# A two-layer attention block: the first layer's opening rebuilt on 128-column tiles, and a modulation chunk moved behind the queries

## The chip, the cores and the metric

The kernel runs on one core of one Trainium2 chip. The number that counts is the device time of one execution in microseconds (us); three runs of the kernel before gave 1213.51, 1214.17 and 1214.43 us, and their median is the time that is compared.

## What is computed

The input is one sequence of 1024 tokens by 1024 channels and two layers. Each layer normalises the tokens, scales and shifts them with a modulation that comes from a second input `c`, projects them to 2736 columns, runs three mixers on these (a retention, a latent attention with rotary positions, a gated linear attention), and adds the gated result. All arithmetic is float32.

```python
c_act = silu(c)
for l in range(2):
    shift, scale, gate = split(c_act @ ada_w[l] + ada_b[l], 3)     # 1024 columns each
    h = rms_norm(x, norm_w[l]) * (1 + scale) + shift
    proj = h @ w_in[l]                  # 1024 x 2736
    r_o = retention(rope(rq), rope(rk), rv)
    m_o = mla(mq, mkv, mkr, ...)        # latent attention
    g_o = gla(gq, gk, gv, gg)           # gated linear attention
    mixed = concat(rms_norm(r_o) * silu(rz), m_o * silu(mz), rms_norm(g_o) * silu(gz))
    x = x + gate * (mixed @ w_out[l])
return rms_norm(x, final_norm)
```

## The kernel before

The activations are kept transposed: `x[k]` is a tile of 128 channels by 1024 tokens, k from 0 to 7, and work goes in two token halves of 512 (`hf`). A float32 product is made of three faster ones (`mm3`, L535 to L537): both operands are split into a rounded part and a remainder (`split`, L435 on ScalarE and L436 on GpSimd or VectorE), and TensorE adds high by high, high by low and low by high. So each projection of 128 output columns is 2 halves x 8 k x 3 matmuls of 512 columns.

`start()` is the opening of the first layer. It is written in a manual schedule: each engine runs its instructions in the order in which the code states them, and waits in that order. It loads x, the tables of positions, the weights of three projections (`rq1`, `rq2`, `rk1`) and 16 tiles of the modulation matrix `ada_w`, all from SyncE's queue, each load 512 KB. Sums of squares over channels go to TensorE as a matmul with ones (`ssq`, L274), and the inverse root is a guess by ScalarE's logarithm and exponential (L424, L425) with one Newton step of three VectorE instructions (L429 to L431). The modulation is made in chunks of 512 columns: chunks 0 and 1 are the shift, 2 and 3 the scale. Chunk 0 is a row on TensorE (`ada_row`, L619, L625). Chunks 1 and 2 are sums over eight row blocks, each multiplied by a column of silu(c) (`ada_steps`: ScalarE L588 and GpSimd L590 for some blocks, VectorE L592 for others), turned into columns by TensorE (L580). Chunk 3 is a product of each column with silu(c) laid along the row (`silrow`), summed by VectorE as it goes (`ada`, L560). GpSimd multiplies x by the inverse root for k 0 to 3 (L320). `h_first` (L798 to L800) then makes h for k 0 to 3 and `make_h` (L666, L672, L679) for k 4 to 7, and the three projections run k 0 to 3 first, then k 4 to 7, half by half. The angles of the rotary tables are made on VectorE at the very start (`trig_angles`), ScalarE takes their sines (`trig`, with two loads of its function table), and SyncE writes the tables to memory (L331).

After the opening only TensorE's order is manual; the other engines' orders come from a planner that places instructions by estimated times. The first layer goes on with `ret_prep` (rotary step on rq and rk, projection `rk2`), `mkv`, `mq0`, `mq1` with their norms (`lat_norm`), `rv`, the keys (`mla_keys`), the retention core, the queries (`mla_queries`, in two parts around `rz0`), `rz1`, then the search for row maxima (`mla_max`), which opens with loads on SyncE's queue (L1251 to L1252, L1198 to L1202). The remaining modulation chunks (gates of both layers, shift and scale of the second) are made one at a time by `ada` at places named by letters: `next_chunk("a")` to `next_chunk("q")` does a chunk if its letter is in `CHUNKS`. A chunk is eight tiles of 256 KB through three buffers, each a load on SyncE's queue (L557) and a product on VectorE (L560), and these products keep their order among themselves.

## Time and profile before

| | |
|---|---|
| time, median of three runs | 1214.17 us |
| the profiled execution's own time | 1211.83 us |
| its span, first to last instruction | 1210.0 us |
| TensorE busy | 1127.9 us, 93% of the span |
| VectorE busy | 853.9 us, 71% |
| ScalarE busy | 564.7 us, 47% |
| GpSimd busy | 559.1 us, 46% |
| mean granted TensorE clock | 0.978 |

The profiled execution is 2.34 us faster than the median of the runs, and 1.83 us of its time lie outside the span. Busy times are sums over the whole span; the opening takes the first 90 us of it and looks different from the rest.

### The profile page before, as it was taken

The numbers are of one execution on the slowest core, as the hardware profiler recorded it, in microseconds if no ns is written. First come the engines' busy times: TensorE is split into PE (matmuls) and PEld (weight loads), VectorE is DVE, ScalarE is ACT, GpSimd is POOL, SyncE is SP. The second block draws the span as 40 slices with busy tenths as digits, with TensorE's granted clock in tenths as the row PEclk, the third lists the DMA queues.
The fourth block names the chain that finished last, engine by engine and source line by source line (L and its number), as shares of the span: only waits on it lengthen the run. The fifth ranks groups of instructions, "written<-read, shape, count | busy, mean of one in ns | idle before, by whom it ended". The sixth has DMA issues, their size and how long they took to land.

```text
span 1210.0 us, 16960 instructions
## 1 busy us (share of the span) xinstructions
PE 1127.9 (93%) x5928; PEld 932.3 (77%) x5928; DVE 853.9 (71%) x1449; ACT 564.7 (47%) x1096; POOL 559.1 (46%) x483
## 2 busy tenths in 40 slices
PE   6599999999999999998998989989999999999996
PEld 1378787778887788886777879777888778888896
DVE  7977779647778666778866565964777766685764
ACT  5432442343453477873444234233345447886421
POOL 3824324443443355683554431544344334568630
PEclk9789999899999999999999999999999999999999
DMA  9806565272117744229451452627212563423722
GB/s 362 283 20 181 172 200 174 88 228 66 41 53 196 177 110 101 68 105 323 146 191 70 121 176 98 221 89 233 61 41 57 162 157 92 105 62 124 276 88 70
DMA packets 65585, 169.01 MB, mean 140 GB/s; under 512 B 10262, under 2 KB 13334, under 8 KB 65500
## 3 DMA queue, kind: packets, MB, share of 16 engines
q1 hardware_dynamic: 65500, 167.93, 45.2%
q8 instruction: 47, 0.77, 0.3%
q14 instruction: 38, 0.31, 0.1%
HBM read 125.36 MB, written 38.41 MB: 135 GB/s over the span
## 4 chain that ended last, share of the span: by engine, by line
PE 59%; DVE 21%; DMA 7%; issue 5%; ACT 4%; POOL 3%; SPq 1%; DVEq 0%; POOLq 0%; ACTq 0%
DMA ada_aw<-awc 3%; PE wo_pspj L535 3%; PE wo_pspj L537 3%; PE wo_pspj L536 3%; PE mhead_psacc L1346 3%; PE mhead_psacc L1344 3%; PE mhead_psacc L1345 3%; DVE ada_aw L560 3%; PE pmz_pspj L535 2%; PE pmz_pspj L536 2%; PE pmz_pspj L537 2%; DVE mmax_mx L1296 2%; PE mhead_pss L1312 2%; PE mhead_pss L1313 2%; DMA aw<-awk 2%
## 5 line engine op out<-in xcount | busy, mean ns | idle before, releaser
L535 PE MATMUL wo_pspj<-gran_mx,wwo_wh 128*128 128x512 f32 (+1 forms) x240 | 89.6, 373 | 6.7 <-DVE ssq_x L1423 3.8
L537 PE MATMUL wo_pspj<-gran_mx,wwo_wl 128*128 128x512 f32 (+1 forms) x240 | 88.4, 368 | 0.0
L536 PE MATMUL wo_pspj<-gran_mx,wwo_wh 128*128 128x512 f32 (+1 forms) x240 | 88.3, 368 | 0.0
L436 POOL TENSOR_TENSOR wwo_wl<-wwo_wst,wwo_wh 128x1024 fp32r<-128x1024 f32 x27 | 69.3, 2569 | 40.1 <-ACT wwo_wh L435 40.0
L1296 DVE TENSOR_REDUCE mmax_mx<-mmax_psmm 128x1 f32<-128x512 f32 (+1 forms) x96 | 57.4, 598 | 31.5 <-PE mmax_psmm L1294 30.4
L1321 POOL TENSOR_TENSOR mhead_wh<-mhead_p,mhead_wh 128x384 fp32r<-128x384 f32 (+1 forms) x48 | 57.9, 1207 | 38.9 <-DVE mhead_wh L1320 38.9
L560 DVE SCALAR_TENSOR_TENSOR ada_aw<-ada_aw,silrow 128x512 f32<-128x512 f32 x64 | 57.2, 919 | 24.6 <-DMA ada_aw<-awc 24.3
L1296 DVE TENSOR_REDUCE mmax_mx<-mmax_psacc 128x1 f32<-128x256 f32 (+2 forms) x96 | 48.9, 509 | 20.8 <-PE mmax_psacc L1294 19.5
L1326 DVE TENSOR_TENSOR mhead_ph<-mhead_pss,mhead_ph 128x512 fp32r<-128x512 f32 x48 | 33.1, 689 | 37.4 <-ACT mhead_pss L1325 36.8
L535 PEld LDWEIGHTS wo_pspj<-gran_mx,wwo_wh 128*128 128x128 f32 x240 | 45.2, 188 | 16.7 <-issue 6.0
L535 PE MATMUL pmz_pspj<-mkh_h,wmz_wh 128*128 128x512 f32 x128 | 52.7, 412 | 0.0
L1321 POOL TENSOR_TENSOR mhead_wl<-mhead_p,mhead_wl 128x128 fp32r<-128x128 f32 (+1 forms) x48 | 35.8, 746 | 34.0 <-DVE mhead_wl L1320 34.0
L537 PEld LDWEIGHTS wo_pspj<-gran_mx,wwo_wl 128*128 128x128 f32 x240 | 45.2, 188 | 7.5
L536 PEld LDWEIGHTS wo_pspj<-gran_mx,wwo_wh 128*128 128x128 f32 x240 | 45.3, 189 | 7.5 <-issue 0.2
L536 PE MATMUL pmz_pspj<-mkh_h,wmz_wh 128*128 128x512 f32 x128 | 50.4, 394 | 0.0
L537 PE MATMUL pmz_pspj<-mkh_h,wmz_wl 128*128 128x512 f32 x128 | 50.1, 392 | 0.0
L639 ACT ACTIVATE ssq_sq<-ssq_x 128x512 f32<-128x512 f32 (+1 forms) x31 | 16.6, 534 | 51.6 <-DVE ssq_x L1423 51.5
L535 PE MATMUL pv_pspj<-wrv_wh,mkh_h 128*128 128x304 f32 x128 | 40.4, 316 | 0.0
L644 DVE TENSOR_TENSOR ssq_sq<-ssq_sq,ssq_sq 128x512 f32<-128x512 f32 (+1 forms) x30 | 30.0, 1000 | 14.4 <-ACT ssq_sq L639 14.4
L1294 PE MATMUL mmax_psmm<-mmax_mxk,mmax_mxq 104*128 104x512 f32 (+1 forms) x96 | 34.8, 362 | 5.6 <-DVE mmax_mx L1296 2.7
L536 PE MATMUL pv_pspj<-wrv_wl,mkh_h 128*128 128x304 f32 x128 | 38.7, 302 | 0.0
L537 PE MATMUL pv_pspj<-wrv_wh,mkh_h 128*128 128x304 f32 x128 | 38.4, 300 | 0.0
(522 smaller groups left out, 4001.1 us busy)
## 6 DMA issues: line engine op xcount, KB each, us to landing
ada_aw<-awc SPq DMA_DIRECT2D x64, 256.0 KB
wwo_wst<-wo SPq DMA_DIRECT2D x32, 512.0 KB
aw<-awk SPq DMA_DIRECT2D x12, 512.0 KB
x<-xT SPq DMA_DIRECT2D x8, 512.0 KB
kn<-mk_ph SPq DMA_DIRECT2D x16, 256.0 KB
kn<-mk_pl SPq DMA_DIRECT2D x16, 256.0 KB
qn<-mq_ph SPq DMA_DIRECT2D x16, 256.0 KB
qn<-mq_pl SPq DMA_DIRECT2D x16, 256.0 KB
```

The lines of the kernel that those rows point to most:

```text
L436: (eng or nc.gpsimd).tensor_tensor(lo, src, hi.bitcast(F32), ALU.subtract)
L535: mm(ps, lh, rh, start=start, stop=False)
L536: mm(ps, lh, rl, start=False, stop=False)
L537: self.last = mm(ps, ll, rh, start=False, stop=stop)
L560: step = nc.vector.scalar_tensor_tensor(v, v, 1.0, self.silrow[:, cs], ALU.mult, ALU.mult, accum_out=t[:, n * j + i:n * j + i + 1])
L1294: nc.tensor.matmul(ps[:, :w], st["q"][0:104, 128 * i:128 * i + 128], st["k"][0:104, 512 * j:512 * j + w], start=True, stop=True)
L1296: nc.vector.tensor_reduce(mx[:, i, j:j + 1], ps[:, :w], AX.X, ALU.max)
L1321: nc.gpsimd.tensor_tensor(pl, p, ph.bitcast(F32), ALU.subtract)
L1326: nc.vector.tensor_tensor(pl, s, ph.bitcast(F32), ALU.subtract)
L1344: mm(acc[:, o], vh, ph, start=(j == 0), stop=False, skip_group_check=True)
L1345: mm(acc[0:64, o], vl, ph, start=False, stop=False, skip_group_check=True)
L1346: mm(acc[:, o], vh, pl, start=False, stop=last, skip_group_check=True)
```

## The change

`start()` is rewritten. The modulation tiles now hold 128 output columns each with all 1024 rows: tile k gives shift and scale of channels 128k to 128k+127, just what `x[k]` needs. The loads come in the order x, then for each k the weights of a projection (k below 3), the scale tile and the shift tile. ScalarE squares all of x, tile by tile; VectorE adds the squares in pairs. The sine work moves from the start to a place behind k = 2, and its last two steps from GpSimd to ScalarE. The root is ScalarE's guess and its square with two VectorE instructions for each half. `column(k)` makes scale (VectorE, a product with `silrow`) and shift (for k below 5 eight one-column matmuls on TensorE, for the others a second VectorE product); `make(k)` makes h for both halves, with `column(k + 1)` between its two parts. Each k's matmuls follow it at once, for those projections whose weights are there (`behind`). GpSimd has no work in the opening. The four old helpers (`ada_steps`, `ada_load`, `ada_row`, `h_first`) go away. `CHUNKS` changes from "acdkno" to "cfgkno": in the first layer the chunks at a (behind `ret_prep`) and d (behind the norm of the latents) go, and there are chunks at f (between the two parts of the queries) and g (behind `rz1`, ahead of `mla_max`); in the second layer, which has two chunks left, they move from a and c to c and f.

```diff
@@ constants @@
-CHUNKS = "acdkno"
+CHUNKS = "cfgkno"
+SHIFT_PE = 5
@@ host_layout @@
-    A["awk"] = ada_w[0].reshape(4, 2, 128, 6, 512)[:, :, :, :3].transpose(3, 0, 2, 1, 4).reshape(3, 4, 128, 1024)
-    A["awc"] = ada_w.transpose(0, 2, 1).reshape(L * 6, 4, 128, D)[3:]
+    A["aws"] = ada_w[0][:, :128 * SHIFT_PE].reshape(KT, 128, SHIFT_PE, 128).transpose(2, 1, 0, 3).reshape(SHIFT_PE, 128, D)
+    A["awc"] = ada_w.transpose(0, 2, 1).reshape(L * 6, 4, 128, D)
@@ start @@
-        dma(pos, A["pos"])
         dma(self.vec, A["vec"])
+        dma(self.cst("ident"), A["cst"][:, 0:128])
         for k in range(KT):
             dma(self.x[k], A["xT"][k])
...
+            if k == 1:
+                dma(pos, A["pos"])
         names = ("rq1", "rq2", "rk1")
-        wst = {}
...
-        aw = self.ada_load((0, 2))
-        for n in names:
-            w_load(n)
-        aw.update(self.ada_load((1, 3)))
+        wst, aw = {}, {}
+        for k in range(KT):
+            if k < len(names):
+                wst[names[k]] = self.sl(name="wst")
+                dma(wst[names[k]], A["wi"][0, MIDX[names[k]]])
+            aw[k] = [self.sl(name="aw") for _ in range(2)]
+            dma(aw[k][1], A["awc"][2 + k // 4, k % 4])
+            dma(aw[k][0], A["aws"][k] if k < SHIFT_PE else A["awc"][k // 4, k % 4])
         self.ahead()
...
+        nc.scalar.preload_act_table_set(TABLES)
...
-        ang, kk, s = self.trig_angles(pos)
-        self.lab = "ssq_"
-        total(square(0), first=True)
-        q1 = square(1, P)
-        q2 = square(2, V)
-        self.trig(ang, kk, s)
-        add(q1, q2)
         o = VO["c"]
         self.silu(self.silc, self.vec[:, o:o + KT], self.sm([128, KT]), self.sm([128, KT]))
...
+        ab = self.sm([128, KT])
+        o = VO["adab"]
+        V.tensor_scalar(ab, self.vec[:, o + KT:o + 2 * KT], 1.0, None, ALU.add)
+        self.lab = "silrow_"
         rows = []
         for hf in range(2):
...
+            dg = self.pt((128, 4, 128), name="dg")
+            rows.append(self.ps())
             V.tensor_tensor(dg, self.cst("ident").unsqueeze(1).to_broadcast([128, 4, 128]),
                             self.silc[:, 4 * hf:4 * hf + 4].unsqueeze(2).to_broadcast([128, 4, 128]), ALU.mult)
...
+            nc.tensor.matmul(rows[hf], self.ones, dg.rearrange("p a b -> p (a b)"), start=True, stop=True)
+        for k in range(0, KT, 2):
+            self.lab = "ssq_"
+            sq = [[self.pt(name="sq") for _ in range(2)] for _ in range(2)]
+            for i in range(2):
+                for hf in range(2):
+                    nc.scalar.activation(sq[i][hf], self.x[k + i][:, hs[hf]], AF.Square)
+            for hf in range(2):
+                V.scalar_tensor_tensor(sq[0][hf], sq[0][hf], EPS * D / 128 if k == 0 else 0.0, sq[1][hf],
+                                       ALU.add, ALU.add)
+                nc.tensor.matmul(ssq[hf], self.ones, sq[0][hf], start=(k == 0), stop=(k + 2 == KT))
+            if k == 0:
+                for hf in range(2):
+                    nc.scalar.copy(self.silrow[:, hs[hf]], rows[hf])
+                ang, kk, s = self.trig_angles(pos)
+        w = {}
+
+        def w_split(n):
+            w[n] = [self.wt(t) for t in ("wh", "wl")]
+            self.lab = "ada_"
+            self.split(*w[n], wst[n], V)
+
+        def column(k):
+
+            self.lab = "ada_"
+            ch, j = k // 4, slice(k % 4, k % 4 + 1)
+            t = self.sm([128, 2])
+
+            def along(i):
+                V.scalar_tensor_tensor(aw[k][i], aw[k][i], 1.0, self.silrow, ALU.mult, ALU.mult,
+                                       accum_out=t[:, i:i + 1])
+            along(1)
+            o = VO["normw"] + k
+            V.scalar_tensor_tensor(self.mod[0][2 + ch][:, j], t[:, 1:2], ab[:, k:k + 1], self.vec[:, o:o + 1],
+                                   ALU.add, ALU.mult)
+            src = t[:, 0:1]
+            if k < SHIFT_PE:
+                ps = self.ps()
+                for i in range(KT):
+                    nc.tensor.matmul(ps[:, 0:1], aw[k][0][:, 128 * i:128 * i + 128], self.silc[:, i:i + 1],
+                                     start=(i == 0), stop=(i == KT - 1))
+                src = ps[:, 0:1]
+            else:
+                along(0)
+            o = VO["adab"] + k
+            nc.scalar.activation(self.mod[0][ch][:, j], src, AF.Identity, bias=self.vec[:, o:o + 1])
+        w_split("rq1")
+        self.lab = "rstd_"
+        ys, zs = [self.pt(name="y") for _ in range(2)], [self.pt(name="rt") for _ in range(2)]
         for hf in range(2):
...
+            nc.scalar.activation(ys[hf], ssq[hf], AF.Ln, scale=1.0 / D)
+            nc.scalar.activation(ys[hf], ys[hf], AF.Exp, scale=-0.5)
+            nc.scalar.activation(zs[hf], ys[hf], AF.Square)
+        column(0)
+
+        def newton(hf):
+            self.lab = "rstd_"
+            V.scalar_tensor_tensor(zs[hf], ssq[hf], -0.5 / D, zs[hf], ALU.mult, ALU.mult)
+            V.scalar_tensor_tensor(ys[hf], zs[hf], 1.5, ys[hf], ALU.add, ALU.mult)
+            self.lab = "mkh_"
+        psum = {(n, hf): self.ps(t) for n, t in zip(names, ("pj", "s", "acc")) for hf in range(2)}
+
+        def mm(n, k):
+            self.lab = f"p{n}_"
+            for hf in range(2):
+                g = self.h[k][hf]
+                cs = slice(128 * k, 128 * k + 128)
+                self.mm3(psum[n, hf], w[n][0][:, cs], w[n][1][:, cs], g[:, 0, :], g[:, 1, :], k == 0, k == KT - 1)
+
+        def make(k):
+
+            self.lab = "mkh_"
+            a, b = self.modcol(0, 8 + k), self.modcol(0, k)
+            ts = [self.pt(name="ht") for _ in range(2)]
+            for hf in range(2):
+                if k == 0:
+                    newton(hf)
+                g = self.h[k][hf] = self.sl((128, 2, 512), F32R, "h")
+                V.scalar_tensor_tensor(ts[hf], self.x[k][:, hs[hf]], a, ys[hf], ALU.mult, ALU.mult)
+                nc.scalar.activation(g[:, 0, :], ts[hf], AF.Identity, bias=b)
+            if 0 < k < KT - 1:
+                column(k + 1)
+            self.lab = "mkh_"
+            for hf in range(2):
+                g = self.h[k][hf]
+                last = V.scalar_tensor_tensor(g[:, 1, :], ts[hf], b, g[:, 0, :].bitcast(F32), ALU.add, ALU.subtract)
+            if k == 0:
+                column(1)
+            return last
+        behind = {0: (("rq1", 0),), 1: (("rq1", 1), ("rq2", 0), ("rq2", 1)),
+                  2: (("rq1", 2), ("rq2", 2), ("rk1", 0), ("rk1", 1), ("rk1", 2))}
         for k in range(KT):
...
+            self.start_last = make(k)
+            if k < 2:
+                w_split(names[k + 1])
+            for n, i in behind.get(k, [(n, k) for n in names]):
+                mm(n, i)
+            if k == 2:
+                self.trig(ang, kk, s)
         for n, o, r in (("r", 0, 32), ("m", 32, 16)):
             self.tab[n] = []
             for t in (kk, s):
...
                     dma(d.rearrange("(a q) c -> q a c", q=r)[:, :, hs[hf]],
                         t[64 * hf + o:64 * hf + o + r, :].unsqueeze(1).to_broadcast([r, 128 // r, 512]))
                 self.tab[n].append(d)
...
         self.rx = {n: self.sl(name=n) for n in names}
...
+        for n in names:
+            for hf in range(2):
                 last = nc.scalar.copy(self.rx[n][:, hs[hf]], psum[n, hf])
...
+            if n == names[0]:
+                self.ahead()
         self.evict = last
@@ trig @@
-        nc.gpsimd.tensor_tensor(kk, kk, kk, ALU.mult)
-        nc.gpsimd.tensor_scalar(kk, kk, -2.0, 1.0, ALU.mult, ALU.add)
+        nc.scalar.activation(kk, kk, AF.Square)
+        nc.scalar.activation(kk, kk, AF.Identity, scale=-2.0, bias=1.0)
@@ ada @@
-    def ada(self, l, ch, tiles=None):
+    def ada(self, l, ch):
...
```

## Rows read from the trace of the kernel before

**Rows 1.** The page's first part: busy time of each engine, its share of the span and its instructions (PEld is TensorE's weight load).
```profile
PE 1127.9 (93%) x5928; PEld 932.3 (77%) x5928; DVE 853.9 (71%) x1449; ACT 564.7 (47%) x1096; POOL 559.1 (46%) x483
```

**Rows 2.** Busy time by stage, all engines: stretch, its length, then busy us (and instructions) of TensorE, its weight loads, VectorE, ScalarE and GpSimd, granted clock, DMA share, GB/s.
```profile
0.00:42.00 42.00, 22.85 (x52) 8.26 (x52) 32.27 (x41) 18.58 (x31) 22.99 (x28) 0.87 0.97 375
42.00:90.00 48.00, 40.65 (x153) 30.31 (x154) 39.96 (x49) 21.08 (x32) 21.30 (x13) 0.87 0.31 91
90.00:170.00 80.00, 77.37 (x404) 66.83 (x403) 56.91 (x90) 27.75 (x56) 26.10 (x17) 0.98 0.54 167
...
215.00:300.00 85.00, 80.08 (x458) 66.68 (x457) 48.90 (x103) 30.31 (x60) 34.56 (x44) 0.96 0.41 121
```

**Rows 3.** TensorE alone in short stretches: stretch, length, busy us (and matmuls), granted clock, DMA share, GB/s.
```profile
41.00:48.80 7.80, 3.72 (x7) 0.55 1.00 268
...
62.70:68.70 6.00, 6.00 (x14) 0.51 0.30 87
68.70:90.00 21.30, 20.91 (x94) 1.00 0.02 2
...
173.70:178.00 4.30, 4.30 (x12) 0.60 0.94 262
```

**Rows 4.** The timeline of the opening: start, duration, engine, line and operation, out<-in; in brackets the idle time before it and what ended it.
```profile
13.62 3.50 PE L274 MATMUL psacc<-ssq_sq,ones 128*128 128x512 f32 x4 [3.40 <-DVE ssq_sq L270]
13.89 2.17 POOL L265 TENSOR_TENSOR ssq_sq<-x 128x512 f32<-128x512 f32 x2 [0.86 <-DMA x<-xT]
...
24.08 0.33 SPq L608 DMA_DIRECT2D aw<-awk  x1
...
25.36 0.33 SPq L608 DMA_DIRECT2D aw<-awc  x1
...
29.79 13.56 POOL L320 TENSOR_TENSOR x<-x,rstd_y 128x512 f32<-128x512 f32 x8
...
32.09 6.63 DVE L592 SCALAR_TENSOR_TENSOR ssq_aacc<-aw,silc,ssq_aacc 128x512 f32<-128x512 f32 x4
...
40.88 0.21 DVE L602 SCALAR_TENSOR_TENSOR mod<-mod,vec 128x4 f32<-128x4 f32 x1
```

**Rows 5.** Who TensorE waited for between 42 and 90 us: us in total, times, longest; and the first matmul of `rk2` on the timeline.
```profile
PE ada_pspj L536 <- DVE mkh_h L800: 6.9, 6, 2.1
...
89.90 0.39 PE L535 MATMUL prk_pspj<-mkh_h,wrk_wh 128*128 128x512 f32 x1
```

**Rows 6.** Durations on the timeline, from stretches where GpSimd does not run beside VectorE: the h instructions, the product of a 128x1024 tile (two in a row), a split's two parts, the Newton instruction, a function table load and a sine.
```profile
8.22 0.63 ACT L388 ACTIVATE trig_kk<-trig_ang 128x512 f32<-128x512 f32 x1
...
9.39 1.28 ACT L390 ACT_TABLE_LOAD   x1
...
25.74 0.69 DVE L431 SCALAR_TENSOR_TENSOR rstd_y<-rstd_rt,rstd_y 128x512 f32<-128x512 f32 x1
...
30.54 1.04 ACT L435 CAST ada_wh<-wst 128x1024 fp32r<-128x1024 f32 x1
...
41.01 1.21 DVE L436 TENSOR_TENSOR ada_wl<-wst,ada_wh 128x1024 fp32r<-128x1024 f32 x1
...
62.55 1.22 DVE L560 SCALAR_TENSOR_TENSOR aw<-aw,silrow 128x1024 f32<-128x1024 f32 x1
63.70 1.22 DVE L560 SCALAR_TENSOR_TENSOR aw<-aw,silrow 128x1024 f32<-128x1024 f32 x1
...
69.78 1.41 DVE L666 SCALAR_TENSOR_TENSOR mkh_ht<-x,mod,rstd_y 128x512 f32<-128x512 f32 x2
70.56 1.39 ACT L672 ACTIVATE mkh_h<-mkh_ht,mod 128x512 fp32r<-128x512 f32 x2 [16.82 <-DVE mkh_ht L666]
```

**Rows 7.** TensorE's pace: pieces of the chain that ended last (start, us, what), a half-clock and a full-clock matmul of the opening, and the eight instructions of four one-column matmuls at either clock (timeline).
```profile
38.78 1.87 PE L580 MATMUL ada_psmm<-ones,ssq_aacc 128*128 128x1 f32 x8 [7.05 <-DVE ssq_aacc L592]
...
64.34 0.43 PE ada_pss L536
...
68.72 0.95 PE L580 MATMUL ada_psmm<-ones,mkh_apart 128*128 128x1 f32 x8
...
76.45 0.23 PE ada_pss L535
```

**Rows 8.** Around the end of the opening, timeline: a copy out of PSUM, the two parts of the split of the weights of `rk2`.
```profile
84.66 0.59 ACT L361 COPY prk_rq<-ada_pspj 128x512 f32<-128x512 f32 x1 [2.13 <-PE ada_pspj L537]
...
85.14 1.05 ACT L435 CAST wrk_wh<-wrk_wst 128x1024 fp32r<-128x1024 f32 x1
...
86.27 2.65 POOL L436 TENSOR_TENSOR wrk_wl<-wrk_wst,wrk_wh 128x1024 fp32r<-128x1024 f32 x1 [1.95 <-ACT wrk_wh L435]
```

**Rows 9.** The chunk at d on VectorE's timeline, its first product and the addition behind its last, and TensorE's wait for the keys behind it (us in total, times, longest); the whole kernel's VectorE idle time before chunk products (us, times).
```profile
160.96 0.69 DVE L560 SCALAR_TENSOR_TENSOR ada_aw<-ada_aw,silrow 128x512 f32<-128x512 f32 x1
...
170.60 2.19 DVE L565 TENSOR_TENSOR ada_sm<-ada_sm 128x4 f32<-128x4 f32 x1
...
PE mk_pspj L535 <- DVE mk_pl L1158: 1.9, 1, 1.9
...
  DMA ada_aw<-awc: 24.3, 19
```

**Rows 10.** Around f and g: TensorE's waits from 215 to 300 us (us in total, times, longest).
```profile
PE mq_pspj L535 <- DVE mq_pl L1158: 2.1, 2, 1.1
PE mmax_psmm L1294 <- DMA mmax_mxq<-qn: 1.4, 1, 1.4
```

More of the change, by code (lines that the diff above doesn't have):

```diff
@@ L272, in total @@
-        def total(q, first=False, last=False):
-            for hf in range(2):
-                nc.tensor.matmul(ssq[hf], self.ones, q[hf], start=first, stop=last)
-        ang, kk, s = self.trig_angles(pos)
-        self.lab = "ssq_"
-        total(square(0), first=True)
-        q1 = square(1, P)
-        q2 = square(2, V)
-        self.trig(ang, kk, s)
-        add(q1, q2)
         o = VO["c"]
         self.silu(self.silc, self.vec[:, o:o + KT], self.sm([128, KT]), self.sm([128, KT]))
-        self.lab = "ssq_"
@@ L291, in start @@
                             self.silc[:, 4 * hf:4 * hf + 4].unsqueeze(2).to_broadcast([128, 4, 128]), ALU.mult)
-            nc.tensor.matmul(ps, self.ones, dg.rearrange("p a b -> p (a b)"), start=True, stop=True)
-            rows.append(ps)
-        self.lab = "ssq_"
-        q3, q4, q5 = square(3), square(4), square(5, P)
-        add(q3, q4)
-        total(q3)
-        q6 = square(6)
-        add(q5, q6)
-        add(q5, square(7))
-        total(q5, last=True)
-        for hf in range(2):
-            nc.scalar.copy(self.silrow[:, hs[hf]], rows[hf])
@@ L304, in start @@
-        ada0, ada2 = self.ada_row(0, aw[0]), self.ada_steps(2, aw[2], (0, 1, 2))
-        for k in range(KT):
-            ada0(k)
-        self.lab = "rstd_"
-        ys, v = [self.pt(name="y") for _ in range(2)], [self.pt(name="rt") for _ in range(2)]
-        for hf in range(2):
-            self.rstd_guess(ys[hf], ssq[hf], float(D), v[hf])
-        for k in range(3):
-            ada2(k)
-        for hf in range(2):
-            self.rstd_newton(ys[hf], v[hf])
-        self.lab = "u_"
-        first, second = range(4), range(4, KT)
@@ L317, in start @@
-        for hf in range(2):
-            for k in first:
-                x = self.x[k][:, hs[hf]]
-                P.tensor_tensor(x, x, ys[hf], ALU.mult)
-        for k in range(3, KT):
-            ada2(k)
-        ada0(KT)
-        ada2(KT)
-        w = {"rq1": w_split("rq1", V)}
+            nc.tensor.matmul(rows[hf], self.ones, dg.rearrange("p a b -> p (a b)"), start=True, stop=True)
[13 more added lines that the diff above has]
+                ang, kk, s = self.trig_angles(pos)
@@ L542, in next_chunk @@
             self.ada(*self.chunks.popleft())
[L544 removed]
+    def ada(self, l, ch):
         nc = self.nc
         self.lab = "ada_"
[L549 to L551 removed]
+        t = self.sm([128, 8])
         for j in range(4):
[L553 to L566 removed]
@@ L568, in ada_steps @@
-    def ada_steps(self, ch, tiles, pool):
-        nc = self.nc
-        main = self.pt(name="aacc") if len(pool) < KT else None
-        part = self.pt(name="apart")
-        def step(k):
-            self.lab = "ada_"
-            if k == KT:
-                ps = self.ps()
-                for j in range(4):
-                    nc.tensor.matmul(ps[:, j:j + 1], (main or part)[:, 128 * j:128 * (j + 1)], self.ones[:, 0:1],
-                                     start=(j == 0), stop=True, skip_group_check=True)
-                self.ada_out(0, ch, ps)
-                return
-            v, c = tiles[k // 2][:, 512 * (k % 2):512 * (k % 2) + 512], self.silc[:, k:k + 1]
-            if k in pool:
-                first = k == pool[0]
-                t = part if first else self.pt(name="prod")
-                nc.scalar.activation(t, v, AF.Identity, scale=c)
-                if not first:
-                    nc.gpsimd.tensor_tensor(part, part, t, ALU.add)
-            else:
-                nc.vector.scalar_tensor_tensor(main, v, c, part if k == len(pool) else main, ALU.mult, ALU.add)
-        return step
+            for i in range(2):
+                cs = slice(512 * i, 512 * i + 512)
+                v = self.gs.tile([128, 512], F32, tag="aw", name=self.nm("aw"), bufs=3)
+                nc.sync.dma_start(v, self.A["awc"][6 * l + ch, j][:, cs])
+                step = nc.vector.scalar_tensor_tensor(v, v, 1.0, self.silrow[:, cs], ALU.mult, ALU.mult,
+                                                      accum_out=t[:, 2 * j + i:2 * j + i + 1])
+                self.tc.keep_in_program_order(step)
```

100 lines of the change are left out of this document (1 added, 99 removed).

## The prediction

> **What bounds the kernel now.** I read the busy shares first [rows 1]: TensorE is busy for 93% of the span and its nearest rival, VectorE, for 71%. Then the same by stage [rows 2]: behind the opening TensorE is busy nearly without a break (77.4 of 80 us from 90 to 170), while in the first 42 us it has 22.9 us of work, most of it sums that only prepare the projections, and up to 90 us it has 40.7 of 48 us, at a clock of 0.87. So the kernel is bound by TensorE except in the opening. The opening's projections are 144 matmuls; at the 0.23 us of [rows 7] they need 33 us, and the next projection, `rk2`, starts at 89.9 [rows 5]. What the opening takes beyond its matmuls is what this change can reach.
>
> Third, the opening's timeline [rows 4]. Data is not what ends last there. x5 has landed at 13.9, and loads of 512 KB follow each other at 1.28 us. The modulation is late: VectorE's last sums take 1.66 us each from 32.1 to 38.7, while GpSimd multiplies x from 29.8 to 43.4. Instructions of that size take 0.67 to 0.70 us on VectorE when GpSimd is idle [rows 6]. The scale is ready at 41.1 and matmuls start at 42. Fourth, TensorE's waits [rows 5]: six waits, 6.9 us, for VectorE's h up to 62.7. Fifth, its clock [rows 3]: 0.55 from 41.0 to 48.8 where TensorE works half the time, 0.51 from 62.7 to 68.7 behind a stretch of waiting, then 1.00. At the low clock (1.2 GHz) a matmul takes 0.43 us, at the high one (2.4 GHz) 0.23 us [rows 7].
>
> **The change part by part: the opening.** I followed the new order on each queue by hand, with durations of before; an instruction begins when its queue and its inputs are free.
>
> Loads: behind x5 come x6, x7, the weights of `rq1`, scale tile 0 and shift tile 0. At 1.28 us each the weights are there at 13.9 + 3 x 1.28 = 17.7 and shift tile 0 at 20.3. The last shift tile is the 21st behind x5: 40.8. The bytes are the same as before; only their order differs.
>
> VectorE: its first piece of the chain is the remainder of `rq1`, at 17.7 + 1.04 (ScalarE's rounding) = 18.8. From there it has in order: 3 remainders of 1.21 = 3.6; 11 products of a 128x1024 tile (8 scales, 3 shifts) at 1.15 from start to start = 12.6; 8 scale columns of about 0.2 (0.21 for the nearest row [rows 4]) = 1.6; 4 Newton instructions of 0.69 = 2.8; 32 instructions of h at 0.67 = 21.4 [rows 6]. Together 42.0. The sines sit on ScalarE between k = 2 and k = 3: two table loads of 1.28 and four passes of about 0.6 make 4.9 us, in which ScalarE can round no h. About 1.8 us of it pass under work that VectorE still has; 3.1 us it waits. So the last h is ready at 18.8 + 42.0 + 3.1 = 63.9. GpSimd has nothing to do in this time, so I take the undisturbed durations. By k this is 4.0 us up to k = 3 and 5.2 us for the ks that need a second product, against 18 x 0.23 = 4.1 us of matmuls: TensorE is fed just slower than it works, and one k of matmuls stays behind the last h: 63.9 + 4.1 + 0.4 for the order within a k = 68.4.
>
> TensorE by itself: 144 x 0.23 = 33.1 and, for five shift columns, 5 x 8 one-column matmuls. Four of these are eight instructions and take 0.95 us at the high clock and 1.87 at the low [rows 7], so a column is 1.9 or 3.75, five are 9.5. From 20.3 this ends at 63, so VectorE ends last, if the clock is high. It will not be all the time: before 20 us TensorE has only the sums of squares, whose four instructions took 3.50 us at 13.6, the low pace [rows 4], and they hold up the root. With half speed until 28 us the same walk ends at 73.2, with half speed until 40 us at 75.0. At 62.7 before, the clock came back after 6 us of steady work [rows 3], and in the new order TensorE is nearly steadily busy from 20.3 on. I take 71, with 68.4 and 75.0 as ends.
>
> The weights of `rk2`: their split follows the two copies of `rq1` out of PSUM, which end its sums 2.7 us (12 matmuls) before the opening ends. Before, 24 matmuls covered it. From 71 - 2.7 come 2 x 0.59, 1.05 and 2.65 [rows 8], so the remainder is there at 73.2, and the third matmul of `rk2`, which needs it, would start at 71.5. That is 1.8 us of waiting; a wait like it cost about 1.5 us more in clock (at 62.7 and 173.7 the clock was 0.51 and 0.60 for 4 to 6 us behind waits [rows 3]; I take less, since it is short). `rk2` is thus as far as if it had started at 71 + 1.8 + 1.5 = 74.3 instead of 89.9: a gain of 15.6 us. The ends: 68.4 with no stall gives 21.5, 75.0 with 3.3 gives 11.6.
>
> What is late next: the rotary steps of rq and rk, of which one ran before the opening ended, now all follow it. That is work of VectorE and GpSimd, and the retention core that needs it comes a hundred microseconds later; TensorE has `rk2`, `mkv`, `mq0`, `mq1` and `rv` until then, and the chunk at a no longer stands on VectorE's queue. I cost it at nothing; without that cover it would be some 6 us. The tables are written to memory later too (sines done at about 44, then eight writes on SyncE's queue, with the next weights and the table's loads behind them); they are due for the rotary step at 70. That too I cost at nothing.
>
> **The chunks.** The chunk at d holds VectorE from 161.0 to about 170.5, its addition takes another 2.2, and TensorE waits 1.9 us for the keys behind it [rows 9] and then runs 4.3 us at 0.60 [rows 3], another 1.7 lost: taking it away gives 3.6 us, at worst 0. Taking away the chunk at a gives nothing by itself: no wait of TensorE ends on it. The new places are f, g, and f in the second layer. Of a chunk, 8 x 0.69 = 5.5 us are work and 24.3/8 = 3.0 us are VectorE's waits for loads. VectorE has room: 48.9 of 85 us are used from 215 to 300 [rows 2]. But behind f stand the queries' remainders, for which TensorE already waits 2.1 us, and behind g the loads of `mla_max` on SyncE's queue, for which it already waits 1.4 us [rows 10]; a load of a chunk tile that waits for its buffer holds up the loads behind it. A single wait of VectorE of some 2 us is covered by the two PSUM tiles of queries (12 matmuls, 2.8 us). So each place costs between nothing and 9.5 - 2.8 = 6.7 us. I take 1.5 each, near the covered end, 4.5 together.
>
> **The sum.** 1211.83 - 15.6 - 3.6 + 4.5 = 1197.1 for the profiled execution. That one lies 2.3 us below the median of the runs shown, so I predict 1199.4, rounded to 1199.
>
> **Rivals.**
> 1. *More is gained* (chance 0.19): the clock is high from the first shift column on, the split of `rk2` stays hidden, f and g cost nothing. 1211.8 - 21.5 - 3.6 + 2.3 = 1189. For it speaks that TensorE's first work comes without long gaps; against it the 0.55 of 41 to 48.8 [rows 3], where it also worked in pieces.
> 2. *The chunks' new places give the gain back* (0.08), the case on the other side: VectorE's queue puts whole chunks ahead of the queries' remainders and the row maxima, and SyncE puts the chunk at g ahead of the loads of `mla_max`. At the bound, 3 x 6.7 = 20 us are lost there, nothing is gained at d: 1211.8 - 15.6 + 20.1 + 2.3 = 1219. It decides from about 5 us per place. Against it: the planner puts other instructions between a chunk's products, and VectorE is half idle there.
> 3. *The clock stays low through the opening* (0.05). Then 144 x 0.43 + 5 x 3.75 = 80.7 us follow 20.3, the opening ends at 101, and 1211.8 + 11.1 + 3.3 - 3.6 + 4.5 + 2.3 = 1229. For it: pieces of work between waits ran at 0.55. Against it: at that pace TensorE would be the slower one and never wait, and steady work brought the clock back [rows 3]. The Trainium skill, "TensorE: Matmul & The Clock Gate", section "HAM oscillation — how this bites in real kernels", has the rule that matmuls in short groups with waits for data between them can run every group at half the clock; by that rule the opening would end at 101, by the rows at 71. The trace agrees with the rule for 41.0 to 48.8 (0.55) and not for the work behind 68.7 (1.00).
> 4. *The opening is shorter but hardly anything moves* (0.04): the rotary steps or the tables, now later, stop TensorE before the retention core, for 12 us or more; about 1212.
>
> **How the numbers follow.** The likeliest case has 0.64. A measurement of this kernel tells about 0.2%, 2.4 us, from no change. The likeliest case and rival 1 are faster, 0.83; between them and rivals 2 and 4 there are mixtures, of which I give 0.03 to faster. Same: 0.04. Slower: 0.10, rivals 2 and 3. The range: the upper end takes the opening's worst bound, d gives nothing, and the places cost 10 us together: 1211.8 - 11.6 + 10 + 2.3 = 1212; the lower is rival 1. I take 1188 to 1211.
>
> **What would show it right or wrong.** In the profile of after: shift tile 0 there at about 20; VectorE busy without long gaps from 19 to 64, its products of 128x1024 at 1.15 and its h instructions at 0.67; a hole of some 3 us at k = 3, with the sines on ScalarE; TensorE's clock at 1.00 from 30 at the latest; the first matmul of `rk2` at 71 to 72 with a short wait for GpSimd behind it; no wait for the keys at the old d; waits of 1 to 2 us at f and g. The prediction is wrong if `rk2` starts outside 68 to 77, or if TensorE's waits between `rk2` and `mla_max` grow by more than 10 us over those of before.

## The result

The changed kernel takes 1198.82 us (median of four runs, 1198.26 to 1202.11) against 1214.3 us for the kernel before on the same chip; the ratio is 0.9875, with an interval of 0.9853 to 0.9897. 1199 was predicted. The profiled execution took 1199.01 us, its span is 1197.2 us.

The busy shares of the profile after, which answer [rows 1]:

```profile
PE 1127.1 (94%) x5968; PEld 940.1 (79%) x5968; DVE 835.3 (70%) x1456; ACT 565.2 (47%) x1102; POOL 528.3 (44%) x459
```

By stage, with the columns of [rows 2] and [rows 3]: the opening to 42 us, its end, the stage behind it, the queries with f and g; then the opening's second half by itself.

```profile
0.00:42.00 42.00, 32.86 (x110) 21.58 (x111) 33.18 (x57) 23.34 (x41) 1.21 (x12) 0.80 0.96 377
42.00:76.00 34.00, 32.30 (x147) 25.87 (x146) 20.18 (x36) 17.82 (x29) 4.10 (x2) 1.00 0.46 131
76.00:156.00 80.00, 80.00 (x423) 69.13 (x423) 53.87 (x70) 31.80 (x63) 34.35 (x21) 1.00 0.45 139
201.00:290.00 89.00, 76.57 (x431) 63.63 (x430) 59.18 (x129) 29.43 (x58) 31.06 (x37) 0.94 0.56 165
...
27.00:34.00 7.00, 6.34 (x22) 5.38 (x22) 6.80 (x13) 3.71 (x7) 0.00 (x0) 0.50 1.03 409
```

TensorE's work is the same. From 76 to 156 us it now has no gap at all; in the queries' stage it is idle for 12.4 of 89 us. The opening is faster although 27 to 34 us run at a granted clock of 0.50, which is the low level (1.2 GHz); 1.00 is the high one (2.4 GHz).

TensorE's waits after, as in [rows 5] and [rows 10] (us in total, times, longest): first 25 to 80 us, then 205 to 290 us. From 80 to 160 us there are none.

```profile
PE ada_pspj L551 <- DVE mkh_h L351: 2.4, 3, 1.2
PE prk_pspj L552 <- POOL wrk_wl L451: 0.9, 1, 0.9
...
PE mq_pspj L550 <- DVE mq_pl L1101: 7.5, 3, 4.5
PE hout_psacc L868 <- DVE mq_rz L872: 2.3, 1, 2.3
```

A ledger of the two profiled executions: each piece is read off the first matmuls that bound it, after minus before. A name such as `mq0` or `gk` stands for the first matmul of that projection.

| piece of the kernel | us | predicted |
|---|---|---|
| up to the first matmul of `rk2` (89.9 to 72.3), with its short stall (+1.25) | -16.3 | -15.6 |
| `mq0` to `rv`, both layers (the chunk at a is gone) | -4.2, -4.9 | 0 |
| `rv` to `gq` (the chunk at d is gone) | -3.6 | -3.6 |
| `rz0` to `gk`, first layer (chunk at f) | +5.7 | +1.5 |
| `gk` to `gv` (chunk at g) | +3.8 | +1.5 |
| `rz0` to `gk`, second layer (chunk at f) | +5.1 | +1.5 |
| all else | +1.6 | 0 |
| sum | -12.8 | -14.7 |

The total came out right, but two terms of it did not: the chunks at a were worth 9.1 us that were not seen, and the new places cost 14.6 us instead of 4.5. The experiments ask for both, and for what paces the opening.

### The profile page after: what moved, and what is told of

The parts are those of the page before. It is cut to its first block, busy times and chain, and to the rows that moved or that the text cites. A ratio compares the mean times of both kernels' runs of the same rounds, so it can differ in the third digit from the quotient of the medians.

```text
span 1197.2 us, 17007 instructions
## 1 busy us (share of the span) xinstructions
PE 1127.1 (94%) x5968; PEld 940.1 (79%) x5968; DVE 835.3 (70%) x1456; ACT 565.2 (47%) x1102; POOL 528.3 (44%) x459
## 4 chain that ended last, share of the span: by engine, by line
PE 69%; DVE 17%; DMA 4%; ACT 4%; issue 3%; POOL 1%; SPq 0%; DVEq 0%; POOLq 0%; ACTq 0%
PE wo_pspj L550 3%; PE wo_pspj L552 3%; PE wo_pspj L551 3%; PE mhead_psacc L1289 3%; PE mhead_psacc L1287 3%; PE mhead_psacc L1288 3%; DVE ada_aw L570 3%; PE pv_pspj L550 2%; PE pmz_pspj L550 2%; PE pmz_pspj L551 2%; DVE mmax_mx L1239 2%; PE pmz_pspj L552 2%; PE pv_pspj L551 2%; PE pv_pspj L552 2%; DMA ada_aw<-awc 2%
## 5 line engine op out<-in xcount | busy, mean ns | idle before, releaser
L550 PEld LDWEIGHTS wo_pspj<-gran_mx,wwo_wh 128*128 128x128 f32 x240 | 45.3, 189 | 17.5 <-issue 7.9
L451 POOL TENSOR_TENSOR wrk_wl<-wrk_wst,wrk_wh 128x1024 fp32r<-128x1024 f32 x3 | 7.7, 2574 | 83.2 <-ACT wrk_wh L450 83.2
L599 DVE TENSOR_TENSOR ssq_sq<-ssq_sq,ssq_sq 128x512 f32<-128x512 f32 (+1 forms) x30 | 30.6, 1020 | 14.6 <-ACT ssq_sq L594 14.6
L550 PE MATMUL pv_pspj<-wrv_wh,mkh_h 128*128 128x304 f32 x128 | 40.7, 318 | 0.0
```

Source lines behind the costliest of these rows:

```text
L451: (eng or nc.gpsimd).tensor_tensor(lo, src, hi.bitcast(F32), ALU.subtract)
L550: mm(ps, lh, rh, start=start, stop=False)
```

## The experiments

All are timed against the kernel before on the same chip; the numbers behind a time are its ratio to that kernel and the interval of the ratio. A stretch of the trace is read from one profiled execution.

**The two halves of the change alone.** First the changed kernel with the old places, then the old kernel with the new ones.

```diff
-CHUNKS = "cfgkno"
+CHUNKS = "acdkno"
```


> The changed kernel with the old places of the chunks (a, c, d, k, n, o): the opening's part of the change alone. Theory P, as predicted: taking away the chunk at a is worth nothing, taking away d is worth 3.6 us, the new places cost 4.5; then this kernel takes about 1198, and the stretch from the first matmul of mq0 to that of rv is the 23.6 us of the changed kernel. Theory B, from the first comparison of traces: the chunk at a holds VectorE when the first half of the latents' norm needs it, ScalarE's copy out of PSUM stands behind that norm, and TensorE waits in both layers; taking it away is worth 4.2 and 4.9 us, d 3.6, and the new places cost 5.7, 4.1 and 5.1. Then this kernel takes 1199 + 4.2 + 4.9 + 3.6 - 14.9 = 1197 less what the later addition of the modulation costs in the output stage (1.1 us), about 1196, with the stretch from mq0 to rv at 27.8 us again. The first matmul of rk2 stays at 72.3 in both.

Measured: 1206.05 us, ratio 0.9936 (0.9911 to 0.9961), above both theories.

```diff
-CHUNKS = "acdkno"
+CHUNKS = "cfgkno"
```


> The kernel before with the new places of the chunks (c, f, g, k, n, o): the chunks' part of the change alone. The first matmul of rk2 stays at 89.9. Theory P: -3.6 + 4.5, about 1215. Theory B: -4.2 - 4.9 - 3.6 + 14.9 + 1.1, about 1217.5, with the stretch from mq0 to rv shortened from 27.8 to about 23.6 us and the stretch from rz0 to gk lengthened from 57.8 to about 63.5. If neither the wait at mq0 goes nor the stretch behind rz0 grows, both changes come from the shift of the opening against the planner's times and not from the places.

Measured: 1217.89 us, ratio 1.0025 (1.0008 to 1.0042). So the opening alone brings about 8 us, the chunks alone lose about 3, and both together gain 15: each half needs the other. The stretch from `mq0` to `rv` shows why: 27.8 us before, 23.6 with the chunks alone, 36.2 with the opening alone, 23.6 with both. First the kernel before in that stretch: VectorE (DVE), then ScalarE, then TensorE on the timeline.

```profile
113.57 2.85 DVE L560 SCALAR_TENSOR_TENSOR ada_aw<-ada_aw,silrow 128x512 f32<-128x512 f32 x1
...
120.98 0.68 DVE L423 TENSOR_SCALAR rstd_rt<-rstd_psmm 128x512 f32<-128x512 f32 x1
...
125.99 0.62 ACT L435 CAST latn_lat<-latn_lf 128x512 fp32r<-128x512 f32 x1 [3.00 <-DVE latn_lf L1104]
126.52 0.59 ACT L702 ACTIVATE pmkv_mq<-pmq_pspj 128x512 f32<-128x512 f32 x1
...
127.16 0.79 PE L535 MATMUL pmq_pspj<-mkh_h,wmq_wh 128*128 128x512 f32 x1 [2.63 <-ACT pmkv_mq L702]
127.75 0.63 PE L536 MATMUL pmq_pspj<-mkh_h,wmq_wh 128*128 128x512 f32 x1
```

The same with the new opening and the chunk still at a:

```profile
110.28 0.69 DVE L570 SCALAR_TENSOR_TENSOR ada_aw<-ada_aw,silrow 128x512 f32<-128x512 f32 x1 [3.27 <-DMA ada_aw<-awc]
...
111.59 0.69 DVE L438 TENSOR_SCALAR rstd_rt<-rstd_psmm 128x512 f32<-128x512 f32 x1
...
117.77 0.79 PE L550 MATMUL pmq_pspj<-mkh_h,wmq_wh 128*128 128x512 f32 x1 [9.65 <-ACT pmkv_mq L657]
```

And in the changed kernel, where the sum that this norm waits for is at 99.41:

```profile
100.47 0.69 DVE L438 TENSOR_SCALAR rstd_rt<-rstd_psmm 128x512 f32<-128x512 f32 x1 [2.90 <-PE rstd_psmm L603]
```

The chunk's products hold VectorE's queue ahead of the norm of the latents; ScalarE's queue holds the norm's result ahead of a plain copy of `mq` out of PSUM; TensorE needs that PSUM tile. TensorE's wait thus names ScalarE and a copy, two queues away from the chunk. It cost 2.6 us and a stretch at the low clock before (0.63 from 127.1 to 131 us), and 9.7 us with the new opening, where the rotary steps stand in front of the same chunk: its first product came 3.6 us ahead of `mq0` before, and 1.5 us behind it here. One product in this chain took 2.85 us where others take 0.69; GpSimd ran a subtraction of its own from 113.47 to 115.88. The Trainium skill, "SBUF — State Buffer", section "SBUF: two separate sides", says that VectorE and GpSimd share a port pair which one instruction holds to its end; this row agrees.

**Do VectorE's waits set the opening's pace?** The chain that ended last, in the changed kernel's opening (start, us, what):

```profile
14.90 5.30 PE psacc L275 x9
...
34.87 0.43 PE ada_pspj L552
...
37.43 0.43 PE ada_pss L552
...
40.12 1.69 PE ada_psmm L305 x16
41.84 0.26 ACT mod L311
42.10 1.28 ACT L403
```

TensorE works at the pace of the low clock (0.43); its shift column 3 is late; ScalarE's sines stand behind that column in its queue, and h of k = 3 behind the sines: VectorE waits 5.2 us there, not 3.1.

```profile
47.81 1.42 DVE L351 SCALAR_TENSOR_TENSOR mkh_h<-mkh_ht,mod,mkh_h 128x512 fp32r<-128x512 f32 x2 [5.22 <-ACT mkh_h L345]
...
66.32 1.42 DVE L351 SCALAR_TENSOR_TENSOR mkh_h<-mkh_ht,mod,mkh_h 128x512 fp32r<-128x512 f32 x2 [0.19 <-ACT mkh_h L345]
```

One run puts the sines ahead of that column (`self.trig` inside `make`, in front of `column(k + 1)`):

```diff
+            if k == 2:
+                self.trig(ang, kk, s)
             if 0 < k < KT - 1:
                 column(k + 1)
...
-            if k == 2:
-                self.trig(ang, kk, s)
```


> The changed kernel with the sine work one place earlier on ScalarE, ahead of column 3 instead of behind it. In the changed kernel ScalarE stands 3.9 us waiting for TensorE's shift of column 3 before it starts the sines, and VectorE then waits 5.2 us for h of k = 3. Theory V, VectorE paces the opening: the wait shrinks to some 1.5 us and the first matmul of rk2 comes 3.5 us earlier, at 68.8, the whole at 1195.5. Theory T, TensorE paces it (it has only 2.4 us of waits between 25 and 72): VectorE's wait goes all the same, but rk2 moves by less than 1.5 us.

Measured: 1199.95 us (0.9887, 0.9859 to 0.9915). The wait at k = 3 falls to 1.33 us, but 2.25 us come at k = 4, where the next shift column is late; `rk2` starts at 70.6, 1.7 earlier, between the two theories, and the stretch from `rz0` to `gk` takes 1.8 us more, so that the total does not move. Two runs take shift columns away from TensorE, the second from the kernel with two chunks under the heads (below):

```diff
-SHIFT_PE = 5
+SHIFT_PE = 3
```


> The changed kernel with shift columns 3 and 4 made by VectorE products too (SHIFT_PE 3 instead of 5): TensorE has 16 one-column matmuls less in the opening (two columns, 1.9 us each at the high clock), VectorE two products of 1.15 us more. Theory T (TensorE at its low clock paces the opening): the first matmul of rk2, at 72.3 in the changed kernel, comes about 2 us earlier, near 70.5, and ScalarE's sines, which waited 3.9 us for a shift column of TensorE, start 2 to 4 us earlier. Theory V (VectorE paces it, as the prediction had it): rk2 comes 2 x 1.15 = 2.3 us later, near 74.6. The time behind the opening is the same in both, 1197 or 1201.

Measured: `rk2` at 70.0, 2.3 earlier although VectorE has 2.3 us more work; in all 1199.31 us (0.988, 0.9842 to 0.9918), the gain given back from the output projection on (+2.5 at the second layer's `rq1`, +2.6 at its `gk`).

```diff
-SHIFT_PE = 5
+SHIFT_PE = 1
```


> As the run with two chunks under the heads, with only shift column 0 on TensorE and seven on VectorE: TensorE has 32 one-column matmuls less (7.6 us at the high clock, 15 at the low), VectorE four products of 1.15 us more, 4.6 us. Theory D (the one-column matmuls behind 20.9 us bring the clock down): 27 to 34 us runs well above 0.50. Theory C (idle time ahead of 14 us does): it stays near 0.50. VectorE then paces the opening: its list of 42.0 us becomes 46.6, last h at 67 to 69, rk2 at 71 to 73 by either.

Measured: `rk2` at 75.3, later than either theory had it; 1190.49 us (0.9817, 0.9785 to 0.985), not told apart from the 1189.28 us of the kernel it was made from. Now TensorE waits for VectorE and for ScalarE's h behind it, 12.6 us in all, and 27 to 34 us stay at 0.50. So with five shift columns it is TensorE's late column that holds the opening up to 47.8 us, and behind that VectorE works up to the last h with 0.2 us of waiting; with one column VectorE's own work paces all of it. Because of TensorE's waits this run doesn't tell why the clock is low.

**Why is the clock low?** Two runs add matmuls that nobody reads, again to the kernel with two chunks under the heads. First ahead of 14 us (`fill(n)` issues n float32 matmuls of ones by a constant tile of 256 columns):

```diff
+        fill(4)
...
                 nc.tensor.matmul(ssq[hf], self.ones, sq[0][hf], start=(k == 0), stop=(k + 2 == KT))
+                if hf == 1 and k == 0:
+                    fill(3)
```


> As the run with two chunks under the heads, with seven matmuls of ones into an unused PSUM tile, four before the first diagonal product and three behind the first pair of squares, so that TensorE does not stand idle up to 14 us. In the changed kernel the granted clock was 0.72 from 14 to 20 us, 1.00 from 20 to 23, 0.68 from 23 to 27 and 0.50 from 27 to 34. Theory C (the low clock of 23 to 38 us comes from TensorE's idle time ahead of 14 us): the sums of squares at 14 us take near 4 us instead of 7.1, the root comes 2 to 3 us earlier, 27 to 34 us runs at 1.00, and the first matmul of rk2, at 72.5, comes near 69 to 70. Theory D (it comes from what TensorE does behind 20.9 us, 32 one-column matmuls and two waits for h): at most the sums of squares are faster, 27 to 34 us stays near 0.50, and rk2 comes at 71 to 73. Total 1186 by C, 1189 by D.

Measured: 1188.8 us (0.9788, 0.9751 to 0.9825), `rk2` at 72.4. TensorE is busy for 8.0 of the first 10 us instead of 5.4, and still 27 to 34 us run at 0.50: the idle start isn't the cause. Then the same kind of matmul among the one-column matmuls (`wide[0]` is a PSUM tile that holds nothing yet):

```diff
...
                 src = ps[:, 0:1]
+                if k < 3:
+                    for _ in range(3):
+                        nc.tensor.matmul(wide[0][:, :256], self.ones, self.reset.rearrange("p c j -> p (c j)"),
+                                         start=True, stop=True)
...
```


> As the run with two chunks under the heads, with three matmuls of ones, 256 columns each, into an unused PSUM tile behind the one-column matmuls of shift columns 0, 1 and 2 (nine in all, by the pace of the sums of squares about 0.45 us each at the high clock and 0.9 at the low). Theory D (the one-column matmuls let the clock fall): 27 to 34 us, at 0.50 in all kernels with this opening so far, now runs near 1.00, the loss of some 6 us there goes, the added work costs 4, and the first matmul of rk2, at 72.5, comes at 70 to 72. Theory E (they are not the cause): 27 to 34 us stays at 0.50, the added work costs up to 8 us of a TensorE that paces the opening, and rk2 comes at 75 to 80.

Measured: 1187.21 us (two runs; 0.9801, 0.9753 to 0.985), `rk2` at 68.8. From 20 to 42 us, first with the wide matmuls, then the kernel they were added to (columns of [rows 2]):

```profile
20.00:42.00 22.00, 20.14 (x118) 17.28 (x118) 20.21 (x35) 12.35 (x20) 0.00 (x0) 1.00 1.03 407
```
```profile
20.00:42.00 22.00, 20.09 (x89) 17.93 (x90) 20.45 (x33) 8.92 (x15) 0.00 (x0) 0.61 1.03 406
```

TensorE is busy for the same 20 us; with the wide matmuls all of it at 1.00 (2.4 GHz), and more work is done in it. `rk2` comes 3.7 us earlier for nine matmuls more than are needed. From 14 to 20 us both kernels ran at 1.00, so the sums of squares make no part of this difference. All eleven other profiles of this opening have 0.50 from 27 to 34; in ten of them TensorE made two shift columns, 16 one-column matmuls, shortly before that, and in the run with one shift column it had long waits instead. The one with the wide matmuls has 1.00. It is one execution, and in the total the run isn't told apart from the kernel it was made from (0.9801 against 0.9797).

One rival is left. The wide matmuls also fill TensorE's waits: the kernel without them waited 1.92 us for shift tile 1, until 23.7 us, and its clock is at 0.50 from 22.2 us on; with them 0.52 us of that wait were left. A long wait isn't needed, though. The changed kernel's clock is 1.00 from 17.7 to 24.4 us and 0.50 from 24.6 to 38, and from 17.7 to 24.4 TensorE waited 0.30 us, ahead of the second column:

```profile
23.03 2.23 PE L305 MATMUL ada_psmm<-silc,aw 128*128 128x1 f32 x16 [0.30 <-DMA aw<-aws]
```

No run fills the waits and leaves the rest as it is. That the wide matmuls went with the high clock is shown; which trait of the old work let it fall is not.

**What does a chunk's place cost?** First f and g empty, the chunks later, behind `gv` (l and m, in the row maxima's stage):

```diff
-CHUNKS = "cfgkno"
+CHUNKS = "cklmno"
```


> The changed kernel with the chunks of the first layer at c, k, l, m, n, o instead of c, f, g, k, n, o (l and m stand between the last gates, mz0 to mz2); in the second layer they are at c and k. Theory S, the place decides: the stretch from rz0 to gk goes back from 63.5 to about 57.8 us and that from gk to gv from 20.2 to 16.1, in both layers the waits for the queries' remainders fall to about 2 us, and l, m and the second layer's k cost up to 1.5 us each: 1199 - 14.9 + 4.5 = 1189. Theory W, VectorE's time is scarce everywhere: a chunk costs 4 to 5 us wherever it stands, 1198 to 1200.

Measured: 1197.25 us (0.9871, 0.9841 to 0.9902). `gk` comes 8.1 us earlier behind `rz0` and `gv` 3.8 behind `gk`, and 11.1 us are lost up to the heads, where TensorE waits for VectorE's row maxima (1.7 us in the changed kernel):

```profile
PE mmax_psmm L1209 <- DVE mmax_sm L1205: 9.9, 2, 6.9
```

Then under the heads of the latent attention, three places or two (the second diff has the same `next_chunk` line):

```diff
+            self.next_chunk({(1, 0): "x", (1, 1): "y", (2, 1): "z"}.get((h, hf), "-"))
...
-CHUNKS = "cfgkno"
+CHUNKS = "cxyzno"
```


> The changed kernel with the chunks at f, g and k moved under the heads of the latent attention (places x, y, z ahead of the score matmuls of three half heads; CHUNKS cxyzno, second layer c and x). In that stage TensorE is busy for 99% and has a long line of work ready. Theory S (a chunk costs what stands behind it on VectorE's queue when TensorE has little work ready): the 5.7 and 4.1 us at f and g go (gk and gv come 8 and 4 us earlier relative to the step before them, as with the late places), second layer's f goes too (5 us), the heads grow by at most 1 us for each chunk; in all 10 to 17 us less than the changed kernel, 1182 to 1189. Theory W (a chunk costs 4 to 5 us wherever it stands, since it takes 9.5 us of a VectorE that is busy for 70%): the heads grow by 4 to 5 us for each chunk and the total stays within 3 us of 1199.

Measured: 1193.36 us (0.984, 0.9811 to 0.9868). f and g save 8.1 and 4.1 us, the heads grow by 10.9.

```diff
-CHUNKS = "cfgkno"
+CHUNKS = "ckxyno"
...
```


> As the run with three chunks under the heads, but the chunk at k stays and two go under the heads (CHUNKS ckxyno, second layer c and k). Theory S: f and g save their 8 and 4 us, the place k costs what it cost in the changed kernel, the second layer's k costs 2 to 3 us in place of f's 5: about 1186 to 1190. Theory W: within 3 us of 1199.

Measured: 1189.28 us (0.9797, 0.9762 to 0.9832). f and g save 5.9 and 3.6, the second layer's f 5.0 (its k costs 2.3), and the heads grow by 2.9. TensorE's waits for the heads' VectorE work, first with three chunks there, then with two:

```profile
PE mhead_psmm L1255 <- DVE mhead_ph L1269: 3.5, 3, 2.1
PE mhead_pss L1255 <- DVE mhead_ph L1269: 1.8, 2, 1.0
```
```profile
PE mhead_psmm L1255 <- DVE mhead_ph L1269: 2.1, 3, 0.9
```

So neither "free under TensorE's long work" nor "4 to 5 us wherever it stands" holds: two chunks cost about 1.5 us each there, a third one about 8. With three, 450 to 480 us ran at a clock of 0.89, with two at 1.00. All these prices are from one execution each.

What f costs is read in the changed kernel: VectorE, then TensorE on the timeline.

```profile
221.23 0.69 DVE L570 SCALAR_TENSOR_TENSOR ada_aw<-ada_aw,silrow 128x512 f32<-128x512 f32 x1 [3.25 <-DMA ada_aw<-awc]
...
222.52 0.68 DVE L1101 TENSOR_TENSOR mq_pl<-mq_pspj,mq_ph 128x512 fp32r<-128x512 f32 x1
...
223.26 0.79 PE L550 MATMUL mq_pspj<-latn_lat,wuq_wh 128*128 128x512 f32 x1 [4.50 <-DVE mq_pl L1101]
```

VectorE waits for the chunk's last tile, the queries' remainder stands behind that product, and TensorE waits 4.5 us for the PSUM tile; then it runs at 0.50 (224 to 228 us). One run keeps VectorE's work and leaves seven of the eight loads at f out, so that the modulation made there is not the one wanted:

```diff
-                v = self.gs.tile([128, 512], F32, tag="aw", name=self.nm("aw"), bufs=3)
-                nc.sync.dma_start(v, self.A["awc"][6 * l + ch, j][:, cs])
+                if not one or (j, i) == (0, 0):
+                    v = self.gs.tile([128, 512], F32, tag="aw", name=self.nm("aw"), bufs=3)
+                    nc.sync.dma_start(v, self.A["awc"][6 * l + ch, j][:, cs])
```


> The changed kernel, in which the chunks at f (both layers) load only the first of their eight tiles and take all eight products on it: VectorE's work stays, seven loads on SyncE's queue and the waits for them are left out (the modulation made there is not the one wanted). f cost about 8 us in the first layer (gk comes 8.1 earlier without f and 5.1 in the second layer). Theory L (the price is the wait for tiles, with the queries' remainders behind it on VectorE's queue): gk comes 5 to 8 us earlier in the first layer, 3 to 5 in the second, TensorE's wait for the queries' remainders falls from 7.5 to about 2 us, total 1187 to 1191. Theory Q (the price is the work of 5.5 us itself): gk comes at most 2 us earlier in each, total 1196 to 1199.

Measured: 1191.77 us (0.9828, 0.9799 to 0.9857). `gk` comes 6.6 us earlier in the first layer, with

```profile
PE mq_pspj L550 <- DVE mq_pl L1102: 3.6, 2, 2.0
```

where 7.5 stood; in the second layer 0.6, though the same wait falls from 5.2 to 2.7. So in the first layer the price is mostly the wait for tiles. In the second the five last products, now in one row, still hold the remainder 4 us. But 1.9 us are also lost there ahead of the first product, with a clock of 0.50 from 769 to 776 us, where the changed kernel had 1.00; so for the second layer this run doesn't decide.

At g it is another thing. VectorE waits hardly 0.2 us for tiles there, and TensorE's wait for `qn` ahead of `mla_max` is 1.1 us, not more than the 1.4 of before. Three products in a row, from 248.16 us on, the last of them long, stand ahead of the step that multiplies the retention's output by its gate (VectorE, changed kernel):

```profile
249.38 1.74 DVE L570 SCALAR_TENSOR_TENSOR ada_aw<-ada_aw,silrow 128x512 f32<-128x512 f32 x1
...
251.05 0.68 DVE L872 TENSOR_TENSOR mq_rz<-hout_psacc,mq_rz 128x512 f32<-128x512 f32 x1
```

TensorE waits 2.3 us for it (`hout_psacc`, above) and then runs at 0.72 (252 to 258 us). No run takes g apart.

**All together.** Two chunks under the heads, three shift columns, earlier sines:

```diff
-CHUNKS = "cfgkno"
+CHUNKS = "ckxyno"
-SHIFT_PE = 5
+SHIFT_PE = 3
...
+            if k == 2:
+                self.trig(ang, kk, s)
             if 0 < k < KT - 1:
                 column(k + 1)
...
-            if k == 2:
-                self.trig(ang, kk, s)
...
+            self.next_chunk({(1, 0): "x", (1, 1): "y", (2, 1): "z"}.get((h, hf), "-"))
```


> As the run with two chunks under the heads, with shift columns 3 and 4 on VectorE and the sines ahead of shift column 3 on ScalarE's queue. Theory T (TensorE paces the opening): rk2 comes at 69 to 70 instead of 72.5, and the total is 1187. Theory V (VectorE, which now has 2.3 us more work and less waiting, paces it by now): rk2 within 1 us of 72, total 1189.

Measured: 1187.29 us, ratio 0.9782 (0.9752 to 0.9812), `rk2` at 69.3. VectorE now runs from 41 to 65 us with 0.2 us of waiting, so it paces the opening. This version beats both kernels. In the total it is not told apart from the one with wide matmuls, which it was not combined with, nor from two chunks under the heads alone (0.9797): what the opening gains here, 3.2 us at `rk2`, is read in the trace and does not show in the time.

## Why the prediction came out as it did

- **The opening, -15.6: right (-16.3, with 1.3 us more in its length and 2.0 less in the stall).** The walk by queues held: from 47.8 on VectorE needs 5.2 us for each k, as in the walk, and TensorE starts `rk2` 4.6 us behind the end of the last h (4.5). What failed is one term, VectorE's 3.1 us of waits: there were 2.0 for the root, whose sums TensorE did partly at the low clock, and 5.2 at k = 3, and the last h came at 67.7 instead of 63.9. Behind it stands a premise, that steady work from 20.3 on brings the clock back, so that TensorE, free by 63, is no limit. The clock came back at about 38, where 30 at the latest was named, and shift columns that ScalarE and VectorE need were late until then. The value of 71 contained a guess for half speed until 28 to 40, and so did not move. With the clock at 1.00 (the run with wide matmuls, one execution) VectorE waited 0.3 for the root and 3.3 at k = 3, the last h came at 64.3 and `rk2` started at 68.8: the walk, and its low end of 68.4. Since the opening's end differs by some 3 us between executions of the same code (last section), the agreement within 1 us is in part luck.
- **The stall of `rk2`, 1.8 + 1.5: too large.** The third matmul waited 0.9 us for GpSimd's remainder and the whole cost 1.25.
- **The rotary steps and the tables, costed at nothing: right only for the chunks as changed.** The cover was named, the chunk at a being gone, and priced at 6 us; with it back, the wait at `mq0` grew from 2.6 to 9.7.
- **"Taking away the chunk at a gives nothing by itself: no wait of TensorE ends on it": wrong, 9.1 us in two layers.** TensorE's wait for `mq0`'s PSUM tile was in the trace of before (2.63 us, put down to ScalarE's copy); behind the copy stood a norm, and behind that the chunk.
- **The chunk at d, -3.6: right** (-3.6, no wait for the keys left).
- **The new places, 1.5 each: mis-sized, 5.7, 3.8 and 5.1.** The range had nothing to 6.7. The covered end was taken since VectorE is half idle and two PSUM tiles hide 2.8 us. At f VectorE's waits for tiles were 3.8 us, near the 24.3/8 = 3.0 of the working, but 3.25 of them came in one piece ahead of the last product, with the remainders behind it on an in-order queue, and the clock fell after TensorE's wait. At g the trace shows products in a row and hardly a wait for tiles. Rival 2, up to 6.7 at each place, had VectorE's queue right and SyncE's at g wrong; at 14.6 us in all it fell short of changing the sign, as d and a gave 12.7 back. TensorE's waits from `rk2` to `mla_max` grew from 9.8 to 12.1 us, not by the 10 us named as a sign of being wrong: the time lost to the clock behind a wait is not in that count.
- **The clock (rival 3).** It was low in a part of the sums of squares (0.55 from 13.9 to 17.5 us) and from about 24 to 38 us, not through the opening. The Trainium skill, "TensorE: Matmul & The Clock Gate", section "HAM oscillation — how this bites in real kernels", puts low stretches down to waits for data between short groups. The traces agree for the stretch behind the 4.5 us wait at f (0.50), not for the fall at about 24.5 us in the changed kernel, where TensorE had waited 0.30 us since 17.7; from 27 to 34 us it was busy for 6.34 of 7 us at 0.50.

Where the total is right by cancellation, it is luck to that extent: 9.1 us missed on one side, 10.1 on the other.

## What to carry to other kernels

Before calling a step on a side engine free, follow each wait of the main engine back through more than one queue: the engine it names may only stand behind the work in question. Price work moved onto an in-order queue by its longest unbroken stretch, waits for data included, and by what stands behind it, not by the mean, and try the place: the same chunk cost from 1.5 us (each of two under the heads) to 8 (at f) here. Two changes that each look small may cover each other, so time both halves alone.

## What the runs showed of the hardware that was not expected

- From 20 to 42 us TensorE was busy for 20 us in both of two kernels. With the shift columns as they are it was granted 0.61, with three wide matmuls behind each of the first three columns 1.00 (one execution each; the wide ones also filled a wait of 1.9 us).
- The clock differs between executions of the same code: in six profiles whose openings are the same, the sums of squares from 14 to 20 us ran at 0.53 to 1.00, and the first matmul of `rk2` lay between 70.5 and 73.8 us. With only the chunks moved the old opening ended at 86.9 instead of 89.9, with 1.00 instead of 0.51 from 62.7 to 68.7. So 2 to 3 us in one profile of the opening are an effect only where the clocks agree, as they do for the run with three shift columns (0.72, 0.68, 0.50 and 0.74 from 14 to 20, 23 to 27, 27 to 34 and 34 to 42 us, the same as in the changed kernel).
